# A Hymba-style decoder layer on one Trainium2 core: value stores and bias repeats on another queue, squares and reloads at other places

## The chip, the cores and the metric

The kernel is one program on one core of a Trainium2 chip. A core has a matrix engine (TensorE, PE in the profile), a vector engine (VectorE, DVE), a scalar engine (ScalarE, ACT), GpSimd (POOL) and SyncE (SP). Each of them runs its own list of instructions in order and waits on semaphores for the others. Transfers between the chip's memory (HBM) and on-chip memory are issued from an engine's list too: here from SP's and from ACT's ("SPq" and "ACTq" in the profile). The transfers themselves run beside the engines.

The metric is the device time of one execution in microseconds (us). The kernel before has a median of 2388.04 us over 3 runs (2383.22 to 2388.99).

## What is computed

One layer of a decoder over 2048 tokens of width 1024, in float32: a root-mean-square norm, one joint projection, two kinds of heads side by side (gated linear attention, and dilated windowed attention with a relative position bias), an output projection, and a feed-forward with squared ReLU.

```python
nx = rmsnorm(h, attn_norm_g)
gq, gk, gv, gr, glow, dq, dk, dv = split(nx @ w_in)          # widths 256,256,512,512,16,512,512,512
o_a = gla_mixer(gq, gk, gv, log_sigmoid(glow @ gla_gate_w2 + b) / 16)   # 4 heads
o_a = rmsnorm_per_head(o_a) * gla_norm_g * silu(gr)
o_b = dilated_mixer(dq, dk, dv, rel_bias)                    # 8 heads, (128,1) (512,4) (2048,16)
h = h + concat([o_a, o_b]) @ w_out
a = square(relu(rmsnorm(h, mlp_norm_g) @ w_ff1))             # 1024 -> 4096
h = h + a @ w_ff2                                            # 4096 -> 1024
y = rmsnorm(h, final_norm_g)
```

## The kernel before

**How a large product is made.** Every float32 operand is split into a high part of reduced precision (`hi`, written by ACT) and the rest (`lo`, by DVE), and a product is three matmuls (`mm3`, lines 66 to 69: high × high, low × high, high × low). On top of that, each large matrix product is cut 2 × 2 and made by Strassen's scheme in Winograd's form: seven products of sums of quarters in place of eight, taken in the order 1, 2, 5, 6, 3, 4, 7. The sums of the tokens' quarters are made once and kept on chip as `TF[j]` (j is the number of the product), a high and a low tile of 128 × 2048 each; those of the weights are made just before use. In the projections every product is left in one of four PSUM banks taken in rotation, and ACT, DVE and POOL carry it into accumulators (`acc` tiles; `CX`, `c11`, `c12`, `c21`, `c22` are their halves).

**Projections (lines 149 to 521, about the first 580 us).** A job is a pair (g, j): 18 groups of seven jobs, 126 jobs. The nine column groups are, in order, `dv`, `gr`, `dq`, `dk`, `dq`, `dk`, `gq`, `gk`, `gv`; groups 0 to 8 are for the first 1024 tokens, 9 to 17 for the second. Groups `dv`, `gr` and `gv` have 256 or 264 columns in each half, and a job is four products (i = 0 to 3, one for each 128 tokens) of 12 matmuls; the others have 128 columns, and a job is one product of 12 matmuls of 512 columns.

- `load_w` (185) asks on SP for a quarter of the next group's weights (tiles `wraw`) as soon as POOL has finished with the old one; `prep` (202 to 214) makes the high and low part (`wcomb`) two jobs ahead of the product, and POOL the sums.
- `product` (275) issues the matmuls; its `rest` evicts (lines 302 to 319); `finish` (235) post-processes a finished quarter and stores it. q and k of the windows go to `qD` and `kD` from ACT (250), q and k of the linear attention from ACT (243), the gates on SP. The values of the windows go to `vD` and, in another arrangement, to `vN`, those of the linear attention to `gvD` (268 to 271): one store for each 128 tokens and column half, on SP for group 0 and on ACT for all others.
- The first 1024 tokens are normalised, transposed and summed at the start. The second 1024 are made ready in the course of groups 1 to 7 by the generator `second_half` (410 to 435), one step each time the job loop meets a number of the list `OTHER` (36). It has four rounds (two blocks of 128 tokens each), and a round has five steps: two loads of x (tile `xp`); two squares on ACT (420), the inverse root and the scaling on DVE (422); the transposes on PE and their evictions by ACT (378, 426) of the first block, and of the second; the sums on DVE and seven stores to `nTD` on SP (429 to 434). `OTHER` puts these steps at jobs 7, 9, 10, 11, 12 in the first round and in the others at jobs 0, 4, 7, 8, 9 counted from the first job of groups 2, 4 and 6 (jobs 14, 28 and 42). All rounds share the tiles `xp` and `bp`.
- In group 8 `reload` (437) brings each of the seven sums back from `nTD` into `xp` or `bp` in turn, and one split (345 on ACT, 346 on DVE; 128 × 2048) rewrites `TF[j]` after its last use by the first half's tokens. Then `bias_rows` (325) makes the relative bias of each distance as one row per head and dilation in `rowD`, in the same tiles.
- `spread_bias` (338) repeats such a row 128 times from `rowD` to `rbD`, two heads at a time: twelve transfers of 384 KB, issued on ACT, at every third job from 72 to 105. The attention reads `rbD` (line 565).

**What sets the order.** The job loop stands under `manual_schedule` for PE, DVE, ACT and POOL. The builder still moves single instructions ahead of work that was written before them; `tc.keep_in_program_order` forbids that for one instruction: it stays behind whatever was written before it on its engine. SP's list and everything outside the block (attention, feed-forward) are ordered by the framework's scheduler. Each transfer signals one of eight completion semaphores in turn, whichever engine issues it, and its issue waits for the transfer before it on the same semaphore.

**Feed-forward.** After the attention (to about 1040 us) and the output projection, whose last row tiles already feed the next norm (`norm_to_T`, which stores the seven sums of transposed rows to `hTD`), the first feed-forward runs (1160 to 1760 us): 32 groups of seven jobs (`jobs1`), 16 groups of columns for the first half of the tokens and 16 for the second, each job 12 matmuls of 512 columns. `reload` (1018) brings a sum from `hTD` into a ring `rb` of tiles and returns a function that splits it into `TF[j]`. The first three (`RELOAD`) are asked for among the output projection's row tiles, the fourth just before the job loop, the next ones each when the one before has been split. The ring has one tile, and a second from the third job on. At the turn to the second half (group 15, jobs 105 to 111) each job is followed by one whole split of its j, and by the request for the load two places on. All large tiles come from one ring of 25 slots (`slot`).

Of the kernel before, what the change touches and what calls it, by code (L numbers as in the profile page):

```python
# [13 lines left out]
AF = mybir.ActivationFunctionType  # L14
# [4 lines left out]
D = 1024  # L19
# [13 lines left out]
XG = (6, 7)  # L33
XSC = {0: (3,), 1: (4,), 2: (5,), 3: (), 4: (6,)}
TOP = (5,)
OTHER = [7, 9, 10, 11, 12] + [14 * k + n for k in (1, 2, 3) for n in (0, 4, 7, 8, 9)]
G0, GE = 8, 56
RELOAD = (10, 11, 12)
BANKS = {"a": 2, "c": 3, "d": 2, "o": 1}
# [2 lines left out]
def emit(tc, a, stop=99):  # L42
    nc = tc.nc
    V, A, G, T, SP = nc.vector, nc.scalar, nc.gpsimd, nc.tensor, nc.sync
# [9 lines left out]
    def slot(name, dt=F32, n=SLOT):  # L54

        return up.tile([128, SLOT], dt, name=name, tag="u", bufs=25)[:, :n]
# [14 lines left out]
    def token_rows(ap, c, row, width=D):  # L71

        return bass.AP(tensor=ap.tensor, offset=ap.offset + c * 128 * row,
                       ap=[[row, 16], [16 * row, 8], [1, width]])

    A.preload_act_table_set("natural_log_exp_and_others")
    ident = const.tile([128, 128], F32, name="ident")
# [54 lines left out]
    gvD = dram.tile([S, 512], F32, name="gvD")  # L132
# [4 lines left out]
    vD = dram.tile([S, 512], F32, name="vD")  # L137
    vN = dram.tile([S, 512], F32, name="vN")
# [3 lines left out]
    hTD = dram.tile([2, 7, 128, 4, 512], F32, name="hTD")  # L142
# [3 lines left out]
    rbD = [dram.tile([8, 128, 384], F32, name=f"rbD{d}") for d in range(3)]  # L146
# [10 lines left out]
    xp, bp, acc = slot("xp"), slot("bp"), [slot("acc") for _ in range(3)]  # L157
# [14 lines left out]
    order = (1, 2, 5, 6, 3, 4, 7)  # L172
# [62 lines left out]
    def finish(g, n, k, i):  # L235

        kind, c0, w = groups[g % NG]
        tb = 2 * (g // NG) + k
        c = C[n][k]
        if w == 128:  # L240
            tk = slice(512 * tb, 512 * tb + 512)
            if kind in ("gq", "gk"):
                A.dma_start((gqD if kind == "gq" else gkD)[n, :, tk], c[:, :512])
                return
            pr = (c0 - (DQ if kind == "dq" else DK)) // 128 + n
            hi = c[:, 512:1024].bitcast(FR)
            A.activation(hi, c[:, :512], AF.Copy)
            V.tensor_tensor(c[:, :512], c[:, :512], hi.bitcast(F32), op=OP.subtract)
            for part in range(2):
                A.dma_start((qD if kind == "dq" else kD)[pr][:, part, tk], c[:, 512 - 512 * part:1024 - 512 * part])  # L250
            return
        t = 4 * tb + i
        tk = slice(t * 128, t * 128 + 128)
        s = c[:, i * w:i * w + w]
        if kind == "gr":
            j = n * w
            m = min(w, 512 - j)
            sg = stage()[:, :m]
            log_sigmoid(sg, s[:, :m])
            A.activation(sg, sg, AF.Exp)  # L260
            V.tensor_tensor(s[:, :m], sg, s[:, :m], op=OP.mult)
            G.tensor_tensor(s[:, :m], s[:, :m], gnB[:, j:j + m], op=OP.mult)
            SP.dma_start(srD[tk, j:j + m], s[:, :m])
            if m < w:
                gate(s[:, m:w], t)
            return
        j = n * w
        q = SP if g == 0 else A
        q.dma_start((vD if kind == "dv" else gvD)[tk, j:j + w], s)
        if kind == "dv":  # L270
            q.dma_start(token_rows(vN[:, j:], t, 512, w), s)

    banks = [0]

# [63 lines left out]
    def spread_bias(d, h):  # L338

        row = rowD[h:, d]  # L340
        A.dma_start(rbD[d][h:h + 2].rearrange("h p n -> p h n"),
                    bass.AP(tensor=row.tensor, offset=row.offset, ap=[[0, 128], [3 * 384, 2], [1, 384]]))

    def split(hi, lo, src):
        A.activation(hi, src, AF.Copy)  # L345
        V.tensor_tensor(lo, src, hi.bitcast(F32), op=OP.subtract)  # L346
# [22 lines left out]
        for cs in (slice(0, 512), slice(512, D)) if t == 0 else (slice(0, D),):  # L369
            V.scalar_tensor_tensor(xs[t][:, cs], x_src(t)[:, cs], X[t], gB[:, cs], op0=OP.mult, op1=OP.mult)  # L370

    def transposed(xt, last=None):
        out = []
        for q in range(2):
            pv = view(ps("cd"[q]), (4, 128))
            for k in range(4):
                of = xt[:, (4 * q + k) * 128:(4 * q + k + 1) * 128]
                T.transpose(pv[:, k, :], last if last is not None and 4 * q + k == 7 else of, ident)
            out.append(pv)
        return out  # L380

# [28 lines left out]
    def second_half():  # L410

        b = [view(bp[:, 512 * q:], (4, 128)) for q in range(4)]
        for i in range(4):
            for k in range(2):
                x_load(8 + 4 * k + i, xp[:, D * k:D * k + D])
            yield
            for k in range(2):
                xt = xp[:, D * k:D * k + D]
                ss = stat()
                A.activation(bp[:, :D], xt, AF.Square, accum_out=ss)  # L420
                r = rstd_of(ss, D)
                V.scalar_tensor_tensor(xt, xt, r, gB, op0=OP.mult, op1=OP.mult)
            yield
            for k in range(2):
                for q, pv in enumerate(transposed(xp[:, D * k:])):
                    A.activation(b[2 * k + q], pv, AF.Copy)
                yield
            (b11, b21, b12, b22), (t2, t4, t3) = b, [view(xp[:, 512 * q:], (4, 128)) for q in range(3)]
            V.tensor_tensor(b12, b12, b11, op=OP.subtract)
            V.tensor_tensor(t2, b22, b12, op=OP.subtract)  # L430
            V.tensor_tensor(t4, b21, t2, op=OP.subtract)
            V.tensor_tensor(t3, t2, b11, op=OP.subtract)
            for j, v in ((1, b11), (2, b21), (5, b12), (6, t2), (3, b22), (4, t4), (7, t3)):
                SP.dma_start(nTD[j - 1][:, :, i * 128:i * 128 + 128], v)
            yield

    def reload(j):
        t = (xp, bp)[order.index(j) % 2][:, :2048]
        SP.dma_start(t, nTD[j - 1].rearrange("p c s -> p (c s)"))
        return lambda: split(*[v[:, :2048] for v in TF[j]], t)  # L440
# [574 lines left out]

    turns = [0]

    def reload(j, half):

        t = rb[turns[0] % len(rb)][:, :2048]  # L1020
        turns[0] += 1
        SP.dma_start(t, hTD[half, j - 1].rearrange("p c s -> p (c s)"))

        def rest():
            if j not in TF:
                TF[j] = [slot(f"hb{j}", FR) for _ in range(2)]
                TB[j] = [view(v, (4, 512)) for v in TF[j]]
            split(*[v[:, :2048] for v in TF[j]], t)

        return rest  # L1030

    def mix_T(t):
        u = view(slot("mx"), (2, D))
# [100 lines left out]
    for at, t in enumerate(tiles):  # L1134
        u, m = nxt
        if at + 1 < NT:
            nxt = mix_T(tiles[at + 1])
        h = u[:, 1]
        p = [ps("a"), ps("a")]
        parts_ = 2 if at < 2 else 1  # L1140
        for q in range(parts_):
            for n in range(2):
                cs = slice(n * 512, n * 512 + 512)
                for c in range(q * CH // parts_, (q + 1) * CH // parts_):
                    mm3(p[n], m[:, 0, c], m[:, 1, c], WO[c][:, 0, cs], WO[c][:, 1, cs], c == 0, c == CH - 1)
                if q == parts_ - 1:
                    V.tensor_tensor(h[:, cs], p[n], u[:, 1, cs], op=OP.add)
        SP.dma_start(hD[t * 128:t * 128 + 128], h)
        if late is not None:
            norm_to_T(*late)  # L1150
        if back:
            back.pop()()
        if at in RELOAD:
            back.append(reload(order[at - RELOAD[0]], 0))
        if at == W1AT:
            load_w1(0)
        if at == W1AT + 1:
            prep1(0)
            prep1(1)
        late = (h, u[:, 0], t)  # L1160
# [123 lines left out]
        tk = slice(i * 128, i * 128 + 128)  # L1284
        mm3(p, l[:, 0, c, tk], l[:, 1, c, tk], r[:, 0, c], r[:, 1, c], n % 8 == 0 and c == 0, n % 8 == 7 and c == 1)

    back = [*back, reload(order[len(RELOAD)], 0)]
    load_w1(1)
    for at in range(7):
        if at == 2:  # L1290
            norm_to_T(*late)
            rb.append(slot("rb"))
        if back:
            back.pop(0)()
        if len(TF) < 7 and not back:
            back.append(reload(order[len(TF)], 0))
        prep1(at + 2)
        product1(at)
    for at in range(7, len(jobs1)):
        if at in (7 * NP - 9, 7 * NP - 8):  # L1300
            back.append(reload(order[at - 7 * NP + 9], 1))
        prep1(at + 2)
        product1(at)
        if jobs1[at][0] == NP - 1:
            back.pop(0)()
            if at + 2 < 7 * NP:
                back.append(reload(order[at + 2 - 7 * NP + 7], 1))
        if at == len(jobs1) - 6:
            for n in range(2):
                load_b(n)  # L1310
                load_a(n)
        if at in (len(jobs1) - 4, len(jobs1) - 2):
            n = (at + 4 - len(jobs1)) // 2
            prep_b(n)
            prep_a(n)
# [81 lines left out]
```

## Time and profile before

| quantity | value |
| --- | --- |
| median of 3 runs | 2388.04 us (2383.22 to 2388.99) |
| the profiled execution's own time | 2389.83 us |
| its span, first to last instruction | 2388.0 us |
| mean granted clock of TensorE | 0.989 |
| DMA | 458.13 MB, mean 192 GB/s |
| PE busy in the projections, 0 to 580 | 528.2 us |
| PE busy in 1500 to 1750 (feed-forward, second half) | 250.00 us of 250 |

The profile is one execution on the chip. A row of waits reads "engine line waited for: us in total, times, longest"; a row of the timeline has the start, the duration, the engine (SPq and ACTq are issues of transfers), the line and the operation "out<-in", and in brackets the idle time before it and what ended it. A row for a line or a tile gives durations in ns (min/median/max), the first and the last start, and the forms; "DMA to landing" is the time from the issue of a transfer to its end. In the rows of windows stand the stretch, its length, PE's busy time with the number of its instructions, the granted clock (1.00 is full), the mean busy share of the 16 DMA engines, and what they moved.

### The profile page before, as it was taken

How to read it: one execution, taken by the hardware profiler on the slowest of the kernel's cores; microseconds unless marked ns; L12 is line 12 of the kernel's file. 1: busy time of each engine (PE TensorE's matmuls, PEld its weight loads, DVE VectorE, ACT ScalarE, POOL GpSimd, SP SyncE). 2: the span in 40 equal slices, each digit the busy share in tenths (PEclk: the TensorE clock that was granted, in tenths of full speed). 3: DMA queues.
4: the chain of work that ended last, by engine and by line, in shares of the span. 5: the costliest groups of instructions: out<-in, count | busy, mean ns of one | idle time of the engine just before them, and what ended most of it. 6: DMA issues, size and time to landing. Idle time of an engine off the chain costs nothing.

```text
span 2388.0 us, 35096 instructions
## 1 busy us (share of the span) xinstructions
PE 2306.9 (97%) x12648; PEld 1988.7 (83%) x12648; DVE 1563.7 (65%) x2879; ACT 1147.0 (48%) x2181; POOL 582.9 (24%) x551
## 2 busy tenths in 40 slices
PE   6999998999999999999999999999999999999998
PEld 5877898779999988888788887888888888888887
DVE  6887675765677778445777778777773455456555
ACT  5565434633766766223555556555553333224323
POOL 5555434546584675100000000000000100001002
PEclk9999999999999999999999999999999999999999
DMA  6457664556667657568654447544467496547653
GB/s 159 122 161 235 202 195 139 194 168 206 207 202 252 208 161 245 172 206 273 202 191 146 154 159 246 178 158 150 146 221 272 150 308 211 175 163 247 218 167 106
DMA packets 342156, 458.13 MB, mean 192 GB/s; under 512 B 19236, under 2 KB 215349, under 8 KB 335710
## 3 DMA queue, kind: packets, MB, share of 16 engines
q1 hardware_dynamic: 313230, 413.15, 53.8%
q10 hardware_dynamic: 28752, 42.74, 5.2%
q8 instruction: 99, 1.62, 0.3%
q14 instruction: 75, 0.61, 0.1%
HBM read 293.51 MB, written 167.02 MB: 193 GB/s over the span
## 4 chain that ended last, share of the span: by engine, by line
PE 73%; DVE 8%; DMA 7%; issue 5%; POOL 3%; ACT 3%; ACTq 0%; SPq 0%; POOLq 0%; DVEq 0%
PE ps_a L67 8%; PE ps_a L68 8%; PE ps_a L69 8%; PE ps_c L67 7%; PE ps_c L69 7%; PE ps_c L68 7%; PE ps_d L67 4%; PE ps_d L68 4%; PE ps_d L69 4%; PE ps_o L67 3%; PE ps_o L68 3%; PE ps_o L69 3%; PE ps_a L674 3%; PE ps_d L655 2%; PE ps_c L633 1%
## 5 line engine op out<-in xcount | busy, mean ns | idle before, releaser
L1231 POOL TENSOR_TENSOR suma<-suma,gs 128x512 f32<-128x512 f32 x16 | 23.3, 1473 | 1149.4 <-ACT scr L1229 1149.3
L346 DVE TENSOR_TENSOR ca<-ra,ca 128x1024 fp32r<-128x1024 f32 x112 | 137.7, 1231 | 157.5 <-ACT ca L345 157.5
L345 ACT ACTIVATE ca<-ra 128x1024 fp32r<-128x1024 f32 x112 | 117.7, 1052 | 216.8 <-PE ps_c L69 167.3
L345 ACT ACTIVATE w1comb<-w1raw 128x512 fp32r<-128x512 f32 x224 | 139.5, 626 | 159.3 <-PE ps_c L69 57.8
L646 ACT ACTIVATE pe<-pe,O 128x256 f32<-128x256 f32 (+1 forms) x384 | 155.8, 454 | 73.7 <-DVE O L645 60.5
L674 PE MATMUL ps_a<-v,pt 128*128 128x65 f32 x1200 | 183.1, 255 | 7.7 <-DVE pt L664 6.6
L674 PEld LDWEIGHTS ps_a<-v,pt 128*128 128x128 f32 x1200 | 178.8, 198 | 11.4 <-DVE pt L664 8.3
L346 DVE TENSOR_TENSOR w1comb<-w1raw,w1comb 128x512 fp32r<-128x512 f32 x224 | 153.9, 690 | 51.3 <-ACT w1comb L345 51.0
L655 PE MATMUL ps_d<-ident,pe 128*128 128x128 f32 x600 | 161.5, 283 | 0.5 <-ACT pe L646 0.5
L645 DVE CUSTOM_DVE_ANT_0 pe<-ps_c,nb 128x256 f32<-128x256 f32 (+1 forms) x384 | 126.1, 361 | 39.5 <-PE ps_d L655 17.9
L202 ACT ACTIVATE wcomb<-wraw 128x512 fp32r<-128x512 f32 (+2 forms) x126 | 96.3, 773 | 110.0 <-PE ps_a L69 21.9
L204 DVE TENSOR_TENSOR wcomb<-wraw,wcomb 128x512 fp32r<-128x512 f32 (+2 forms) x84 | 99.9, 1194 | 71.6 <-ACT wcomb L202 71.4
L345 ACT ACTIVATE cb<-rb 128x1024 fp32r<-128x1024 f32 x56 | 59.4, 1061 | 168.7 <-PE ps_o L68 99.2
L67 PE MATMUL ps_c<-hb,w1comb 128*128 128x512 f32 x336 | 131.7, 392 | 2.4 <-ACT hb L345 2.4
L68 PE MATMUL ps_c<-hb,w1comb 128*128 128x512 f32 x336 | 131.6, 392 | 1.0 <-DVE w1comb L346 1.0
L69 PE MATMUL ps_c<-hb,w1comb 128*128 128x512 f32 x336 | 131.1, 390 | 0.0
L67 PE MATMUL ps_c<-cb,ca 128*128 128x512 f32 x336 | 130.8, 389 | 0.0
L68 PE MATMUL ps_c<-cb,ca 128*128 128x512 f32 x336 | 130.8, 389 | 0.0
L69 PE MATMUL ps_c<-cb,ca 128*128 128x512 f32 x336 | 130.8, 389 | 0.0
L655 PEld LDWEIGHTS ps_d<-ident,pe 128*128 128x128 f32 x600 | 112.0, 191 | 1.0 <-ACT pe L646 0.7
L94 POOL TENSOR_TENSOR stats<-stats,mhalf 128x1 f32<-128x1 f32 (+1 forms) x64 | 47.2, 743 | 254.1 <-DVE stats L93 208.9
L346 DVE TENSOR_TENSOR cb<-rb,cb 128x1024 fp32r<-128x1024 f32 x56 | 68.2, 1223 | 61.0 <-ACT cb L345 60.9
(351 smaller groups left out, 7342.4 us busy)
## 6 DMA issues: line engine op xcount, KB each, us to landing
ra<-actD SPq DMA_DIRECT2D x56, 1024.0 KB, 6.8
actD<-acc SPq DMA_DIRECT2D x192, 256.0 KB, 2.3
rb<-w_ff SPq DMA_DIRECT2D x72, 512.0 KB, 4.8
w1raw<-w_ff SPq DMA_DIRECT2D x32, 1024.0 KB, 7.6
k<-kD SPq DMA_DIRECT2D x16, 1024.0 KB, 8.9
rb<-hTD SPq DMA_DIRECT2D x14, 1024.0 KB, 5.7
wraw<-w_in SPq DMA_DIRECT2D x48, 256.0 KB, 3.3
boD<-O SPq DMA_DIRECT2D x8, 1056.0 KB, 4.5
```

Source lines behind the costliest of these rows:

```text
L67: T.matmul(out, sh, mh, start=first, stop=False)
L68: T.matmul(out, sl, mh, start=False, stop=False)
L69: T.matmul(out, sh, ml, start=False, stop=last)
L94: G.tensor_tensor(r2, r, mhalf[:, :n], op=OP.pow)
L202: A.activation(hi, src, AF.Copy, scale=sc)
L204: V.tensor_tensor(lo, src, hi.bitcast(F32), op=OP.subtract)
L345: A.activation(hi, src, AF.Copy)
L346: V.tensor_tensor(lo, src, hi.bitcast(F32), op=OP.subtract)
L645: V.tensor_tensor_reduce(p, s, bias, scale=1.0, scalar=BIG, op0=OP.add, op1=OP.min, accum_out=nm)
L646: A.activation(p, p, AF.Exp, bias=nm, scale=-1.0)
L655: T.transpose(pb[:, i * 128:i * 128 + 128], src, ident)
L674: T.matmul(self.b.opsum[:, n % 4], self.pt[:, i * 128:i * 128 + 128], self.b.v[:, blk, cols], start=first, stop=last)
```

## The change

In the projections:

- The squares, and the first transpose of each block in `second_half`, are kept in program order. `OTHER` puts the steps of rounds 2 to 4 at jobs 0, 6, 9, 10, 11 in place of 0, 4, 7, 8, 9.
- The values' second arrangement `vN` is still stored per 128 tokens, now always on SP. `vD` and `gvD` are stored once for four blocks (512 tokens, 512 KB), after the fourth, on SP.
- The twelve repeats of the biases are issued on SP and kept in program order there.

In the first feed-forward:

- The second tile of the ring and a further tile (`rt`) exist before the job loop; the fourth, fifth and sixth reload are asked for before it, the seventh after the second job's split.
- A split is two halves of 1024 columns. At the turn the fourteen halves are spread over jobs 106 to 116, the n-th at job 106 + 4n/5; the first two loads are asked for at job 103, and that of place k + 2 after the second half of place k.

```diff
-OTHER = [7, 9, 10, 11, 12] + [14 * k + n for k in (1, 2, 3) for n in (0, 4, 7, 8, 9)]
+OTHER = [7, 9, 10, 11, 12] + [14 * k + n for k in (1, 2, 3) for n in (0, 6, 9, 10, 11)]
...
-        q = SP if g == 0 else A
-        q.dma_start((vD if kind == "dv" else gvD)[tk, j:j + w], s)
         if kind == "dv":
-            q.dma_start(token_rows(vN[:, j:], t, 512, w), s)
+            SP.dma_start(token_rows(vN[:, j:], t, 512, w), s)
+        if i == 3:
+            SP.dma_start((vD if kind == "dv" else gvD)[512 * tb:512 * tb + 512, j:j + w].rearrange("(i p) n -> p i n", i=4),
+                         c[:, :4 * w].rearrange("p (i n) -> p i n", i=4))
...
-        A.dma_start(rbD[d][h:h + 2].rearrange("h p n -> p h n"),
-                    bass.AP(tensor=row.tensor, offset=row.offset, ap=[[0, 128], [3 * 384, 2], [1, 384]]))
+        tc.keep_in_program_order(
+            SP.dma_start(rbD[d][h:h + 2].rearrange("h p n -> p h n"),
+                         bass.AP(tensor=row.tensor, offset=row.offset, ap=[[0, 128], [3 * 384, 2], [1, 384]])))
...
-    def transposed(xt, last=None):
+    def transposed(xt, last=None, pin=False):
...
-                T.transpose(pv[:, k, :], last if last is not None and 4 * q + k == 7 else of, ident)
+                ins = T.transpose(pv[:, k, :], last if last is not None and 4 * q + k == 7 else of, ident)
+                if pin and q + k == 0:
+                    tc.keep_in_program_order(ins)
...
-                A.activation(bp[:, :D], xt, AF.Square, accum_out=ss)
+                tc.keep_in_program_order(A.activation(bp[:, :D], xt, AF.Square, accum_out=ss))
...
-                for q, pv in enumerate(transposed(xp[:, D * k:])):
+                for q, pv in enumerate(transposed(xp[:, D * k:], pin=True)):
...
-    def reload(j, half):
+    def reload(j, half, t=None):
-
-        t = rb[turns[0] % len(rb)][:, :2048]
-        turns[0] += 1
-        SP.dma_start(t, hTD[half, j - 1].rearrange("p c s -> p (c s)"))
+        if t is None:
+            t = rb[turns[0] % len(rb)]
+            turns[0] += 1
+        SP.dma_start(t[:, :2048], hTD[half, j - 1].rearrange("p c s -> p (c s)"))
...
-            split(*[v[:, :2048] for v in TF[j]], t)
-
-        return rest
+            for cs in (slice(0, 1024), slice(1024, 2048)):
+                split(*[v[:, cs] for v in TF[j]], t[:, cs])
+                yield
+
+        return rest()
...
-    back = [*back, reload(order[len(RELOAD)], 0)]
+    rb.append(slot("rb"))
+    back = [*back, reload(order[3], 0), reload(order[4], 0), reload(order[5], 0, slot("rt"))]
...
-            rb.append(slot("rb"))
         if back:
-            back.pop(0)()
-        if len(TF) < 7 and not back:
-            back.append(reload(order[len(TF)], 0))
+            list(back.pop(0))
+        if at == 1:
+            back.append(reload(order[6], 0))
...
+    first, parts_at = 7 * (NP - 1), {}
+    for n in range(14):
+        parts_at.setdefault(first + 1 + n * 4 // 5, []).append(n // 2)
+    halves, begun = {}, set()
     for at in range(7, len(jobs1)):
-        if at in (7 * NP - 9, 7 * NP - 8):
-            back.append(reload(order[at - 7 * NP + 9], 1))
+        if at == first - 2:
+            halves.update({n: reload(order[n], 1) for n in range(2)})
...
-        if jobs1[at][0] == NP - 1:
-            back.pop(0)()
-            if at + 2 < 7 * NP:
-                back.append(reload(order[at + 2 - 7 * NP + 7], 1))
+        for n in parts_at.get(at, ()):
+            next(halves[n])
+            if n in begun and n + 2 < 7:
+                halves[n + 2] = reload(order[n + 2], 1)
+            begun.add(n)
```

More of the change, by code (lines that the diff above doesn't have):

```diff
@@ L1151, in emit @@
         if back:
-            back.pop()()
+            list(back.pop())
         if at in RELOAD:
```

## The prediction

> **What bounds the kernel now.** I read the page first, then busy time by stage, then the losses in short windows, then what each late instruction waited for.
>
> ```profile
> span 2388.0 us, 35096 instructions
> PE 2306.9 (97%) x12648; PEld 1988.7 (83%) x12648; DVE 1563.7 (65%) x2879; ACT 1147.0 (48%) x2181; POOL 582.9 (24%) x551
> 60.00:580.00 520.00, 489.64 (x2948) 0.98 0.59 177
> 580.00:1160.00 580.00, 564.66 (x4137) 0.99 0.67 215
> 1160.00:1760.00 600.00, 595.11 (x2614) 1.00 0.51 171
> 1760.00:2388.00 628.00, 618.98 (x2729) 1.00 0.61 205
> ```
>
> In a window row stand the stretch, its length, PE's busy time with its instructions, the granted clock, the DMA share and GB/s. PE sets the time everywhere: 2306.9 of 2388.0 us. The change leaves its matmuls alone, so only PE's losses can move: idle time, and busy time at a lowered clock. The projections after their start (60 to 580) idle 30.4 us, the first feed-forward (1160 to 1760) 4.9. For a shorter window I count the loss as idle time plus busy time times (1 − clock).
>
> ```profile
> 130.00:150.00 20.00, 17.82 (x65) 0.83 0.39 100
> 210.00:215.00 5.00, 2.94 (x17) 1.00 0.75 262
> 235.00:245.00 10.00, 6.68 (x22) 0.66 0.59 194
> 280.00:290.00 10.00, 8.13 (x66) 1.00 0.47 139
> 320.00:335.00 15.00, 12.16 (x98) 1.00 0.42 125
> 360.00:385.00 25.00, 16.44 (x107) 0.80 0.77 227
> 385.00:390.00 5.00, 5.00 (x43) 1.00 0.29 74
> 445.00:460.00 15.00, 12.94 (x54) 1.00 0.64 199
> 1165.00:1180.00 15.00, 12.55 (x48) 0.89 0.66 206
> 1465.00:1480.00 15.00, 12.56 (x54) 1.00 0.68 253
> ```
>
> The losses are, in order: 2.18 + 17.82 × 0.17 = 5.2; 2.06; 3.32 + 6.68 × 0.34 = 5.6; 1.87; 2.84; 8.56 + 16.44 × 0.20 = 11.8; none at 385, which shows the full pace of 256-wide matmuls (43 in 5 us, 0.116 us each); 2.06; 2.45 + 12.55 × 0.11 = 3.8; 2.44 us. Their causes, by the views of waits:
>
> ```profile
> ACT bp L420 <- DMA xp<-x: 15.7, 6, 5.3
> PE ps_c L378 <- DVE xp L422: 2.1, 1, 2.1
> PE ps_d L378 <- DVE stats L93: 3.3, 1, 3.3
> 133.69 1.06 ACT L420 ACTIVATE bp<-xp 128x1024 f32<-128x1024 f32 x1 [3.34 <-DMA xp<-x]
> ```
>
> The first, second and third windows are one thing: ACT runs in order and stands at a square whose tokens are still landing (15.7 us in six waits); the evictions and weight preparations behind it are late, and so are the scaled rows that PE transposes.
>
> ```profile
> PE ps_c L67 <- ACT wcomb L202: 5.2, 1, 5.2
> PE ps_o L67 <- ACT acc L315: 3.3, 1, 3.3
> ACT wcomb L202 <- DMA vN<-acc: 11.9, 1, 11.9
> ACT acc L315 <- DMA vD<-acc: 9.1, 1, 9.1
> L341 ACTq DMA_DIRECT2D rbD<-rowD x12: 538/608/1131, 350.2 to 380.0; - x12
> DMA to landing us min/median/max: 4.6/7.9/13.6
> ```
>
> The waits of PE and ACT in 345 to 385 and the repeats' own view. The window at 360 is ACT's queue of transfers: all twelve bias repeats are issued between 350.2 and 380.0 us among the second token half's value stores, each takes 7.9 us (median) to land, and a value store that must wait for an earlier landing holds ACT for 9.1 and 11.9 us. PE then waits 5.2 and 3.3 us, and its clock falls.
>
> ```profile
> PE ps_c L67 <- ACT hb L345: 2.4, 1, 2.4
> PE ps_d L67 <- ACT hb L345: 1.3, 1, 1.3
> ACT hb L345 <- DMA rb<-hTD: 5.3, 3, 3.9
> ```
>
> At 1165 and 1465 PE waits for whole splits (ACT hb) of reloaded operands, some of whose loads had not landed.
>
> **The change, part by part.** It removes 48 transfers: 64 stores of attention and GLA values, 128 rows each, become 16 of 512 rows. In the built program ACT's transfers go from 189 to 113, SP's from 1013 to 1041; bytes and PE's instructions stay.
>
> 1. Squares. In the built order the squares of the second token group go from position 124 of ACT's list to 195, those of the fourth from 256 to 268 (about seven products, some 20 us), while their loads stay; those of the third keep their place, but its loads come about 6.7 us earlier, since the transposes ahead of them do. The waits were 3.34 and up to 5.3 us, well below both shifts, so the losses 5.2 + 2.1 + 5.6 = 12.9 us can go. The bound on the gain is 12.9. From the other side: the pinned transposes sit in PE's order, where nothing overtakes them, so a late row now stops PE itself; I keep half, 6, as the poor end. I take −11, near the full end, as 20 us stands against 5.3.
>
> 2. Value stores and repeats off ACT. The two ACT waits can't arise on ACT any more; bound 11.8. Before the wait DVE and ACT were already close behind PE, so I take −10.5; poor end −8.5, PE's two waits alone.
>
> 3. Where the repeats go. They now stand on SP at every third product, some 380 to 520 us, each beside weight loads and q and k stores.
>
> ```profile
> L565 SPq DMA_DIRECT2D nb<-rbD x24: 319/427/538, 549.2 to 593.8; - x24
> L250 ACTq DMA_DIRECT2D qD<-acc x16: 326/326/475, 428.3 to 492.7; - x16
>   ACT acc L307: 5.6, 2
> DMA to landing us min/median/max: 2.0/3.5/6.0
> SPq L185 <- POOL wraw L210: 30.8, 4, 14.1
> ```
>
> These are the first reads of the repeats, the views of tile qD from 400 to 580 (who waited for it, its landings), and SP's waits from 200 to 300. ACT L307 overwrites a tile that a q store is reading; it waited 5.6 us in two cases, and the 445 window lost 2.06. With repeats in the same stretch these landings lengthen. Of twelve repeats perhaps four meet a q or k pair at up to 2.06 us each: 0 to +8. I take +3, three at half of that. SP itself stands up to 14.1 us before a weight load until POOL frees the raw tile, so a repeat or value store behind it waits too; nothing needs a repeat before its reads at 549 us. The tiles behind the joined value stores are written again two to three jobs later (a job of four 256-wide products is 48 matmuls of 0.116 us, 5.6 us), so they have 11 us; cover gone, ACT waits as above.
>
> The Trainium skill, "DMA: Bandwidth & Descriptors", section "Issuing engines are not separate DMA queues", says that transfers started by any of the engines share the same 16 DMA engines, and that spreading the issuing saves only the issue time. By that alone part 2 would gain nothing beyond ACT's issues; the waits for landing (9.1 and 11.9 us) speak against it here, since they block evictions, which on SP's queue they do not.
>
> 4. Later transposes. The fourth group's transposes come 42 matmuls later than before (0.225 us each at 512 columns, as in the row of 1500 below): 9.4 us for its seven stores and for the reloads of group 8 behind them.
>
> ```profile
> 270.05 0.34 SPq L439 DMA_DIRECT2D xp<-nTD  x1
> 282.31 1.94 ACT L345 ACTIVATE tb<-xp 128x2048 fp32r<-128x2048 f32 x1
> 279.63 1.06 ACT L202 ACTIVATE wcomb<-wraw 128x1024 fp32r<-128x1024 f32 x1 [7.51 <-POOL wraw L208]
> xp<-nTD SPq DMA_DIRECT2D x4, 1024.0 KB, 7.9
> ```
>
> The reload at 270.05 moves to about 279.5 (SP's queue adds some 2: 282), lands near 288, and its split stands in ACT's order right behind the evictions that ended at 282.3 less the wraw wait: up to 8.5 us of ACT held. PE rotates four banks, three products (12 × 0.116 us each) ahead of an eviction, 4.2 us; with the hold at 7, as the place on SP is known to some 2 us: +3. Ends 0 (the split slides without stopping PE) and +6 (half clock too).
>
> 5. Weight loads of group 8 now stand ahead of the fourth group's stores on SP; ACT's 7.51 us wait on the raw weights goes, with the 1.87 us window. −1.9, ends 0 and −1.9. The 320 window (DVE with splits) is untouched, and a later chain gives it less room; 0, in the range of part 4.
>
> 6. First feed-forward, start. Two more tiles hold reloads, three are requested before the first product instead of one after the other: the 3.8 us window goes but for the split's own time. −3, ends 0 and −3.8 (the extra tiles come out of the same ring of 25, and could delay the last row tile's load or the second weight tile).
>
> 7. Turn of the halves. Splits come as fourteen halves over eleven products instead of seven whole ones over seven.
>
> ```profile
> DMA to landing us min/median/max: 4.8/6.7/8.5
> 1500.00:1750.00 250.00, 250.00 (x1105) 1.00 0.46 156
> ```
>
> The landings are those of the reloads from 1440 to 1510. A product is 12 × 250/1105 = 2.71 us. ACT and DVE are freed between halves, but a load is asked for only two or three products (5.4 to 8.1 us) ahead of its first half, against landings of 4.8 to 8.5: an ACT wait of up to 3 us stays. −1.5, ends −2.4 and +1.
>
> Attention, the output projection and the second feed-forward keep their order: 0.
>
> Sum: −11 − 10.5 + 3 + 3 − 1.9 − 3 − 1.5 = −21.9. The profiled execution took 2389.83 us (span 2388.0), 1.8 above the runs' median of 2388.04: 2389.8 − 21.9 = 2367.9, and I say 2367.5. All good ends: −12.9 − 11.8 + 0 + 0 − 1.9 − 3.8 − 2.4 = −32.8, 2357. All poor ends: −6 − 8.5 + 8 + 6 + 0 + 0 + 1 = +0.5, 2390.
>
> **Rivals.**
>
> A. Everything gained, nothing new: −30 to −33, about 2358. For it: the repeats have some 30 us to spare, and the split could slide. Against: the later reload has a chain of its own (stores, load, split) that the rows show without slack. 15%.
>
> B. The squares' stall only moves to the reload: ACT held 8.5 us at 288, PE through its banks, then at half clock as in the 235 window (2.3 us): +8.5 + 2.3 = 11 instead of 3. −21.9 + 8 = −14, 2376. For it: reloads and splits are chained through two tiles. Against: PE's bank slack. 14%.
>
> C. The transfers decide, not the queue: repeats at 7.9 us hold back whatever they meet, so part 2 is given back as waits elsewhere. −21.9 + 10.5 = −11.4, 2378.5. Against it: in 360 to 385 the DMA share was 0.77, not full, and what waited there was ACT's order. 10%. The Trainium skill's rule on shared DMA engines (part 3) would have it come out this way.
>
> D. Slower: SP becomes the blocked queue. A transfer that must wait for an earlier one's landing held ACT; the same wait now holds SP, whose next entry is a weight load. Each repeat would cost one late load (the 280 window, 1.87) and one late q or k store (half of 2.06): 12 × 2.9 = 35 in place of part 3's 3: −21.9 + 32 = +10, 2400. It decides where SP's hold exceeds the lead of the weight loads, which are asked for most of a group ahead (seven products, 19 us at 128 columns); the longest landing of a repeat was 13.6 us, seen with eight in flight, so I doubt it. 7%.
>
> E. The edits don't take, and the scheduler's order swallows them. The built order shows them moved; only the feed-forward part could vanish. 2% for nothing.
>
> **Chances.** The forecast, −16 to −27, has 52%; A to E as above. This kernel's measurement tells about 0.3% (7 us) from no change. Faster by more than that: all of the forecast and A, most of B and C: 0.84. Within: the rest of B and C, and E: 0.08. Slower: D and mishaps of its kind: 0.08. The range leaves out D and A's edge: 2356 to 2385; the likeliest one's own is 2362 to 2374.
>
> **What would show it.** Right: in 130 to 245 no wait of ACT for xp<-x above 1 us and PE busy in the 5 us windows there; between 350 and 385 no ACT wait on a value store's landing; PE at clock 1.00 near 370; PE full at 1165 to 1180. Part 4: ACT waiting for xp<-nTD near 288. Part 3: ACT L307 waiting for q or k stores at 400 to 520, more than 5.6 us in all. D: POOL waiting for wraw loads there, and SP's queue held at repeats. It would be wrong if 60 to 580 idles as much as before at other places, or if a stage that I set to 0 (attention) moves.

## The result and the profile after

The changed kernel takes 2374.87 us (median of 4 runs, 2372.88 to 2376.36), the kernel before 2388.51 us in the runs beside it. The ratio is 0.9944 with a 95% interval of 0.9923 to 0.9965: about 13.6 us faster, where 20.5 were forecast. The profiled execution has a span of 2374.6 us, 13.4 below that of before. The measured time lies in the range of 2356 to 2385, but just beyond the 2362 to 2374 that were called likeliest.

PE's list holds 9168 matmuls of lines 67 to 69 in every kernel here. The builder lets some of them change places, but over a few products only: in the projections each window below holds the same matmuls, by line and bank, in every kernel (but for four at job 70 in e1). At the limits in the feed-forward up to 11 are exchanged for others of the same shape. So windows can be cut at the i-th matmul, which is the same amount of work in each trace. The first fence has such windows of the kernel before, the second those of the changed kernel. Row by row they are the jobs from 14 to 21, 21 to 27, 27 to 35, 35 to 42, 42 to 49, 49 to 70, 70 to 77, 77 to 90, 90 to 98, 98 to 105, then the first 14 jobs of the first feed-forward and its jobs 103 to 120. The length is what matters here.

```profile
130.37:158.71 28.34, 25.92 (x101) 0.88 0.46 132
158.71:178.90 20.19, 19.80 (x86) 1.00 0.63 202
178.90:203.45 24.55, 24.55 (x110) 1.00 0.70 216
203.45:226.80 23.35, 21.30 (x102) 1.00 0.82 243
226.80:253.06 26.26, 22.94 (x94) 0.87 0.66 189
253.06:362.64 109.58, 104.86 (x771) 1.00 0.67 208
362.64:416.08 53.44, 44.88 (x340) 0.90 0.47 136
416.08:459.82 43.74, 41.68 (x177) 1.00 0.55 171
459.82:483.53 23.71, 23.71 (x101) 1.00 0.71 239
483.53:505.02 21.49, 19.59 (x85) 1.00 0.54 171
1150.87:1194.43 43.56, 41.11 (x179) 0.96 0.64 205
...
1436.51:1486.07 49.56, 47.12 (x205) 1.00 0.67 232
```

```profile
130.75:154.65 23.90, 22.35 (x95) 1.00 0.59 165
154.65:175.30 20.65, 20.03 (x86) 1.00 0.56 178
175.30:209.02 33.72, 27.67 (x117) 0.95 0.68 191
209.02:231.61 22.59, 21.11 (x101) 1.00 0.71 216
231.61:250.75 19.14, 19.14 (x86) 1.00 0.76 227
250.75:362.45 111.70, 107.05 (x780) 0.98 0.62 195
362.45:404.28 41.83, 41.38 (x340) 1.00 0.41 117
404.28:446.33 42.05, 41.43 (x176) 1.00 0.66 202
446.33:476.56 30.23, 26.41 (x103) 0.94 0.76 236
476.56:499.20 22.64, 20.27 (x85) 1.00 0.66 200
1145.05:1184.19 39.14, 39.14 (x179) 1.00 0.87 279
...
1426.27:1473.65 47.38, 46.57 (x205) 1.00 0.66 233
```

Read the lengths against each other. At the stalls that the change aimed at, time was gained: 4.4 us at jobs 14 to 21, 0.8 at 35 to 42 and 7.1 at 42 to 49 (squares), 11.6 at 70 to 77 (ACT's queue), 4.4 and 2.2 in the feed-forward. ACT has no wait for x left between 60 and 300 us. But two stretches that were at full pace have become slow: jobs 27 to 35 take 9.2 us more, jobs 90 to 98 take 6.5 more.

The first of the two, by PE's waits from 182 to 202 us and the timeline of DVE (start, duration, line), first in the changed kernel, then two rows of the one before:

```profile
PE ps_o L67 <- DVE acc L305: 3.7, 1, 3.7
```

```profile
188.90 1.78 DVE L320 TENSOR_TENSOR acc<-acc 128x512 f32<-128x512 f32 x1
190.60 1.78 DVE L434 TENSOR_TENSOR xp<-bp 128x512 f32<-128x512 f32 x1
192.42 1.65 DVE L435 TENSOR_TENSOR xp<-bp,xp 128x512 f32<-128x512 f32 x1
193.99 0.68 DVE L436 TENSOR_TENSOR xp<-xp,bp 128x512 f32<-128x512 f32 x1
194.59 1.28 DVE L248 TENSOR_TENSOR acc<-acc 128x512 f32<-128x512 f32 x2
195.79 1.00 DVE L305 TENSOR_TENSOR acc<-ps_o,acc 128x512 f32<-128x512 f32 x1
```

```profile
188.83 1.02 DVE L304 TENSOR_TENSOR acc<-ps_o,acc 128x512 f32<-128x512 f32 x1
...
197.29 1.79 DVE L430 TENSOR_TENSOR xp<-bp 128x512 f32<-128x512 f32 x1
```

Line 305 is the eviction (304 before) of the bank that PE needs. In DVE's list it now stands behind the last three sums of the second token group (434 to 436, places 210 to 212, the eviction at 215). Before, it stood ahead of them (place 210, the sums, then lines 430 to 432, at 219 to 221). The group's squares start some ten products later than they did (at 170.80 us, 133.69 before) and the first of its four sums about five; these three come about two products earlier. PE stands 3.7 us and then runs at a lowered clock (0.95 over the window). The same holds in every kernel here: the seven with the sums ahead of this eviction take 32.8 to 35.1 us for jobs 27 to 35, the seven with the sums behind it 24.6 to 25.5.

The second, by the waits of ACT and PE of the changed kernel from 455 to 495 us, and then the landings of k's transfers (tile kD) from 400 to 580, first in the changed kernel, then in the one before:

```profile
ACT acc L308 <- DMA kD<-acc: 5.6, 1, 5.6
...
ACT acc L308 <- DMA qD<-acc: 2.2, 1, 2.2
```

```profile
PE ps_o L67 <- ACT wcomb L202: 1.7, 1, 1.7
```

```profile
DMA to landing us min/median/max: 2.1/5.2/10.1
```

```profile
DMA to landing us min/median/max: 2.0/2.7/4.2
```

These transfers land in 5.2 us (median) in place of 2.7. One of those counted is a load of k; the stores alone, 11 and 10 of 16 with a landing on record, took 5.0 and 2.7. ACT, which overwrites the tile, stands 5.6 us for one of them, and PE waits for weights (wcomb) that ACT makes in the same order. The waits don't price each link of this chain; that the repeats set it off is shown by e1.

### The profile page after: what moved, and what is told of

Read it like the earlier page. It is cut to its first block, busy times and chain, and to the rows that moved or that the text cites. A ratio compares the mean times of both kernels' runs of the same rounds, so it can differ in the third digit from the quotient of the medians.

```text
span 2374.6 us, 35066 instructions
## 1 busy us (share of the span) xinstructions
PE 2303.8 (97%) x12648; PEld 1985.9 (84%) x12648; DVE 1563.5 (66%) x2893; ACT 1148.6 (48%) x2195; POOL 577.9 (24%) x551
## 4 chain that ended last, share of the span: by engine, by line
PE 80%; DVE 8%; DMA 4%; issue 4%; ACT 2%; POOL 2%; SPq 0%; ACTq 0%; POOLq 0%; DVEq 0%
PE ps_a L67 8%; PE ps_a L69 8%; PE ps_a L68 8%; PE ps_c L68 7%; PE ps_c L69 7%; PE ps_c L67 7%; PE ps_d L67 4%; PE ps_d L69 4%; PE ps_d L68 4%; PE ps_a L678 3%; PE ps_o L67 3%; PE ps_o L68 3%; PE ps_o L69 3%; PE ps_d L659 2%; PE ps_c L637 2%
## 5 line engine op out<-in xcount | busy, mean ns | idle before, releaser
L1238 POOL TENSOR_TENSOR suma<-suma,gs 128x512 f32<-128x512 f32 x16 | 23.3, 1472 | 1142.8 <-ACT scr L1236 1142.8
L67 PE MATMUL ps_a<-wcomb,tb 128*128 128x256 f32 (+1 forms) x336 | 99.1, 295 | 10.5 <-DVE acc L305 5.5
```

The costliest lines, as they stand in the source:

```text
L67: T.matmul(out, sh, mh, start=first, stop=False)
```

## The experiments

Times are medians; the kernel before ran beside each of them. The table has the length of each stretch of PE's list in the profiled execution, by jobs, in us; FF is the first 14 jobs of the first feed-forward, turn its jobs 103 to 120.

| kernel | median | 14-27 | 27-35 | 35-49 | 14-49 | 49-70 | 70-77 | 77-90 | 90-105 | FF | turn |
| --- | --- | --- | --- | --- | --- | --- | --- | --- | --- | --- | --- |
| before | 2388.5 | 48.5 | 24.6 | 49.6 | 122.7 | 109.6 | 53.4 | 43.7 | 45.2 | 43.6 | 49.6 |
| changed | 2374.9 | 44.6 | 33.7 | 41.7 | 120.0 | 111.7 | 41.8 | 42.1 | 52.9 | 39.1 | 47.4 |
| e1 | 2380.2 | 46.6 | 32.8 | 41.8 | 121.1 | 119.0 | 42.9 | 43.3 | 46.8 | 39.1 | 47.0 |
| e2 | 2379.0 | 44.5 | 34.8 | 41.7 | 121.0 | 110.5 | 43.4 | 42.1 | 53.5 | 39.9 | 47.1 |
| e3 | 2376.6 | 48.4 | 24.6 | 48.3 | 121.3 | 108.4 | 41.8 | 42.1 | 52.1 | 39.2 | 47.0 |
| e4 | 2374.7 | 47.4 | 25.5 | 44.7 | 117.5 | 112.1 | 41.8 | 42.1 | 51.3 | 39.3 | 47.0 |
| e5 | 2378.4 | 45.0 | 33.7 | 41.8 | 120.4 | 112.3 | 41.8 | 44.7 | 50.4 | 39.4 | 47.0 |
| e6 | 2372.6 | 48.8 | 25.5 | 43.3 | 117.6 | 111.7 | 41.7 | 42.0 | 52.0 | 39.5 | 47.0 |
| e7 | 2377.9 | 44.9 | 35.1 | 41.8 | 121.7 | 110.0 | 41.8 | 42.0 | 52.5 | 39.1 | 47.7 |
| e8 | 2384.0 | 45.0 | 33.6 | 44.7 | 123.2 | 109.2 | 41.8 | 42.1 | 51.7 | 45.2 | 49.1 |
| e9 | 2376.5 | 44.9 | 34.9 | 41.8 | 121.6 | 111.5 | 46.2 | 45.3 | 45.3 | 39.2 | 47.0 |
| e10 | 2375.5 | 45.8 | 25.4 | 47.6 | 118.8 | 111.6 | 45.2 | 45.1 | 46.7 | 39.1 | 47.0 |
| e11 | 2369.9 | 47.4 | 25.5 | 44.8 | 117.6 | 112.3 | 41.8 | 44.5 | 45.5 | 39.1 | 47.0 |
| e12 | 2371.0 | 49.0 | 25.4 | 44.4 | 118.8 | 111.9 | 41.7 | 43.2 | 45.3 | 39.1 | 47.0 |

### Repeats back on ACT (e1)

```diff
-        tc.keep_in_program_order(
-            SP.dma_start(rbD[d][h:h + 2].rearrange("h p n -> p h n"),
-                         bass.AP(tensor=row.tensor, offset=row.offset, ap=[[0, 128], [3 * 384, 2], [1, 384]])))
+        A.dma_start(rbD[d][h:h + 2].rearrange("h p n -> p h n"),
+                    bass.AP(tensor=row.tensor, offset=row.offset, ap=[[0, 128], [3 * 384, 2], [1, 384]]))
```

> The changed kernel (2374.9 us) with the twelve bias repeats back on ACT, not pinned; value stores stay joined on SP. Theory: the repeats are what held ACT at jobs 70 to 72 (their landings, 7.9 us median, against 2 for a value store), so most of the 12.3 us gained there is lost again (+8 to +12), while the 6 us lost at jobs 90 to 101, where q and k stores wait, come back: 2377 to 2381. Rival: the many value stores held ACT; then jobs 70 to 72 stay good and the 6 us come back: about 2369.

It took 2380.2 us. ACT's and PE's waits of this kernel from 320 to 400 us:

```profile
ACT acc L316 <- DMA rbD<-rowD: 11.8, 2, 9.7
```

```profile
PE ps_o L67 <- ACT acc L316: 6.7, 1, 6.7
```

With no value store on ACT's queue the repeats hold ACT by themselves, now a little earlier (jobs 49 to 70 lose 7.3 us, 70 to 77 lose 1.1). So 8.4 of the 11.6 us are lost again. Jobs 90 to 105 are back to 46.8. So the repeats are the cause of most of the old stall and, on SP, of the new one at jobs 90 to 105.

### Value stores back on ACT (e2)

```diff
+        q = SP if g == 0 else A
+        q.dma_start((vD if kind == "dv" else gvD)[tk, j:j + w], s)
         if kind == "dv":
-            SP.dma_start(token_rows(vN[:, j:], t, 512, w), s)
-        if i == 3:
-            SP.dma_start((vD if kind == "dv" else gvD)[512 * tb:512 * tb + 512, j:j + w].rearrange("(i p) n -> p i n", i=4),
-                         c[:, :4 * w].rearrange("p (i n) -> p i n", i=4))
+            q.dma_start(token_rows(vN[:, j:], t, 512, w), s)
```

> The changed kernel with the value stores as before (one for each 128 tokens, on ACT but for group 0), the repeats on SP. Theory: without repeats among them they land in about 2 us and hold ACT for little, also with 48 more transfers: 2374 to 2378, no ACT wait above 3 us between 345 and 385. Rival: the value stores themselves are the stall, which returns: 2384 to 2387.

2379.0 us. The stall does not return: jobs 70 to 77 take 43.4, 1.6 more, and ACT waits for no landing between 320 and 400. Its profiled execution, the longest of its five, is 6.8 us longer than the changed kernel's, and 5.3 of that lie in the attention (364.6 us against 359.3). That is above the scatter of this stage (last section), but the engines' lists in it are not quite those of the other kernels; what made it longer is not shown. Joining these stores is worth 1 to 2 us where they are made, which single profiles hardly tell from scatter.

### Squares undone (e3)

```diff
-OTHER = [7, 9, 10, 11, 12] + [14 * k + n for k in (1, 2, 3) for n in (0, 6, 9, 10, 11)]
+OTHER = [7, 9, 10, 11, 12] + [14 * k + n for k in (1, 2, 3) for n in (0, 4, 7, 8, 9)]
-                tc.keep_in_program_order(A.activation(bp[:, :D], xt, AF.Square, accum_out=ss))
+                A.activation(bp[:, :D], xt, AF.Square, accum_out=ss)
-                for q, pv in enumerate(transposed(xp[:, D * k:], pin=True)):
+                for q, pv in enumerate(transposed(xp[:, D * k:])):
```

> The changed kernel with the squares' and transposes' pins and the offsets as before. Theory from the two traces, job by job: part 1 gained 4.4 + 1.5 + 6.6 at jobs 15 to 20, 37 to 39 and 44 to 46, and lost 10.1 at jobs 27 to 32, so undoing it costs about 2 to 3 us: 2377, with PE full from 180 to 200 and the three old stalls back. Rival: the loss at jobs 27 to 32 comes from something else (the value stores on SP), and undoing costs the 11 us of the prediction: 2386.

2376.6 us, as the theory had it. Jobs 27 to 35 fall to 24.6, and the old stalls return. Jobs 14 to 49 differ by 1.3 us in all, not by 11, and that is within the scatter: the kernels that share the changed kernel's steps there (changed, e1, e2, e5, e8, e9) took 120.0 to 123.2.

### Pins with the old offsets (e4), and only round 2 at them (e6)

```diff
-OTHER = [7, 9, 10, 11, 12] + [14 * k + n for k in (1, 2, 3) for n in (0, 6, 9, 10, 11)]
+OTHER = [7, 9, 10, 11, 12] + [14 * k + n for k in (1, 2, 3) for n in (0, 4, 7, 8, 9)]
...
+OTHER = [7, 9, 10, 11, 12, 14, 18, 21, 22, 23] + [14 * k + n for k in (2, 3) for n in (0, 6, 9, 10, 11)]
```

> The changed kernel with the pins but the offsets 0, 4, 7, 8, 9. Theory: the pins alone end the waits for x (a load of about 7 us against four jobs, 10.9 us), and the loss at jobs 27 to 32 is round 2's four sums on DVE standing ahead of an eviction at the start of group 4; two jobs earlier they don't meet it: -5 to -10, 2365 to 2370. Rival: the pinned transposes themselves stop PE wherever they stand, and the time stays within 3 us of 2375; a second rival, that six products are needed because x lands late: ACT waits for xp<-x above 1 us and 2378 or more.

> The changed kernel, pins kept, with only the second round at the old offsets 0, 4, 7, 8, 9 (rounds 3 and 4 at 0, 6, 9, 10, 11). Theory: the stall at jobs 27 to 35 (9 us) belongs to round 2's sums on DVE two jobs later, the new stall at jobs 35 to 42 of the run with all offsets old (2.9 us) to round 3's squares two jobs earlier; so here 27 to 35 in 25.5 us, 35 to 42 in 22.6 us, 21 to 27 in 23.4: 5 to 6 us below the changed kernel in the profile, 2369. Rival: round 3's place depends on round 2's, and 35 to 42 loses 3 us all the same: 2372.

e4 took 2374.7 us by the median (2369.6 to 2380.6), no better than the changed kernel, though its profiled execution was 6.8 shorter. In its profile the stall at jobs 27 to 35 goes as the theory says (25.5), and ACT waits for x 2.6 us in two cases, 1.6 the longest (the fence below), against 15.7 us in six before: the second rival's wait is there, but small, and its time is not reached. But new losses come before and behind. PE's waits of e4 from 155 to 235 us:

```profile
PE ps_a L67 <- ACT wcomb L202: 3.1, 2, 2.8
PE ps_c L380 <- DVE xp L426: 3.0, 2, 2.8
```

ACT's waits of e4 from 60 to 300 us:

```profile
ACT bp L424 <- DMA xp<-x: 2.6, 2, 1.6
```

The pinned transposes now come before DVE has scaled their rows. e6 (2372.6 us) shows the same at round 2: 8 us gained at jobs 27 to 35, 4.2 lost at 14 to 27, 1.6 at 35 to 49. Jobs 35 to 42, where the theory had 22.6 us, took 23.3. Of five arrangements of these steps (changed, e3, e4, e6, e10) none takes jobs 14 to 49 below 117.5 us, 2.5 less than the changed kernel.

### Squares pinned alone (e7)

```diff
-                for q, pv in enumerate(transposed(xp[:, D * k:], pin=True)):
+                for q, pv in enumerate(transposed(xp[:, D * k:])):
```

> The changed kernel with the squares pinned but not the transposes. Theory: the waits for x stay gone (jobs 14 to 21 in 23.9 us, 42 to 49 in 19.1), and the scheduler spreads the transposes again, so the stall at jobs 27 to 35 shrinks by 3 us or more: 2366 to 2372. Rival: the DVE work of the later squares alone makes the stall, and 27 to 35 stays at 33 us: 2374 to 2376.

The rival holds: 35.1 us at jobs 27 to 35, with the same wait of 3.7 us for DVE's line 305, and 2377.9 us. The pinned transposes are not what stops PE there. What is left are the moved steps of round 2, as e6 shows, which put the three sums ahead of the eviction.

### Feed-forward as before (e8)

The functions and loops of the first feed-forward are those of the kernel before.

> The changed kernel with the first feed-forward's reloads as before. Theory: its start loses 4.4 us and its turn 2.2 us, nothing else moves: 2381 to 2382 by the median, 6.6 more in the profile. Rival: the gain at the start came from the earlier stages (the last row tiles), and only the turn's 2.2 us come back: 2377.

2384.0 us. The start loses 6.0, the turn 1.7, nothing else in the feed-forward moves: more than the 6.6 that the two traces showed, from the same places. Jobs 35 to 49 take 3.0 us more than in the changed kernel, with the same steps there: so much can a stretch differ from profile to profile.

### Repeats in the gate group, two a job (e5) and three a job (e9)

```diff
-        if 7 * NG + 8 <= at < 7 * NG + 44 and at % 3 == 0:
-            spread_bias(2 - (at - 7 * NG - 8) // 12, (at - 7 * NG - 8) // 3 % 4 * 2)
+        if 7 * NG + 8 <= at < 7 * NG + 14:                    # e9: < 7 * NG + 12, three in place of two
+            for n in (2 * (at - 7 * NG - 8), 2 * (at - 7 * NG - 8) + 1):
+                spread_bias(2 - n // 4, n % 4 * 2)
```

> The changed kernel with the twelve repeats, still on SP and pinned, two at each of jobs 71 to 76 (the gate group, which stores no q or k) in place of every third job from 72 to 105. Theory: the 6 to 7 us lost at jobs 90 to 101 come from repeats among q and k stores, so they go here (jobs 90 to 98 in 23.7 us, not 30.2), and the gate group, where the DMA share was 0.39, takes the repeats for less than 2 us: 2367 to 2370. Rival: it is the bytes and the queue wherever they stand (4.7 MB in 35 us): jobs 70 to 77 lose 5 us or more, by late weights behind the repeats on SP: 2373 or more.

> The changed kernel with three repeats at each of jobs 71 to 74, so that in the built list of SP all twelve stand ahead of the weight loads of the next groups (in the run with two a job the last two stood 25 entries later and were issued at 466 us). Theory: with no repeat left at 460 to 480, where 2 MB of k for the attention are already being loaded, jobs 90 to 105 take 45.5 us or less (52.9 in the changed kernel, 50.4 with two a job) and jobs 70 to 90 gain or lose under 2: 2368 to 2371. Rival: the k loads alone saturate the transfers there, or the gate group pays: within 2 us of 2375.

In e5 (2378.4 us) jobs 90 to 98 are at 23.7 us, as expected, and 70 to 77 pay nothing. But 77 to 90 and 98 to 105 give back 6.7. The last two repeats stand 30 places further down in SP's list (issued at 466.5 and 467.2 us) and fall among the attention's first loads of k (2 MB). The transfers issued in 460 to 485 (KB each, median us to landing), and POOL's waits of e5 from 455 to 495:

```profile
k<-kD SPq DMA_DIRECT2D x1, 1024.0 KB, 8.8
wraw<-w_in SPq DMA_DIRECT2D x3, 256.0 KB, 10.0
rbD<-rowD SPq DMA_DIRECT2D x2, 384.0 KB, 9.3
```

```profile
POOL wraw L208 <- DMA wraw<-w_in: 9.9, 1, 9.9
```

A weight load lands in 10.0 us here (median of three); over the projections of before it was 3.3. In e9 (2376.5 us) no repeat is left there, and jobs 90 to 105 take 45.3, as the theory had it; but the rival is right too, for the gate group pays 4.4 us and the next jobs 3.3. POOL's and PE's waits of e9 from 355 to 440:

```profile
POOL wraw L208 <- DMA wraw<-w_in: 20.6, 3, 14.7
```

```profile
PE ps_d L227 <- POOL acc L319: 3.8, 1, 3.8
```

Nine of the repeats (3456 KB) are issued within 10.5 us, from 381.0 us on. POOL then stands 14.7 us for a weight load, and a sum that the gates need is behind it in POOL's list.

### Three a job and another round 2 (e10)

```diff
+OTHER = [7, 9, 10, 11, 12, 14, 18, 22, 23, 24] + [14 * k + n for k in (2, 3) for n in (0, 6, 9, 10, 11)]
```

> As the run with three repeats a job, and round 2 at jobs 14, 18, 22, 23, 24: squares two products earlier, transposes and sums one earlier than in the changed kernel. In the built lists round 2's four evictions and last three sums then stand nearly where the kernel before had them (177 and 208 to 211 on DVE, in place of 192 and 198 to 200). Theory: jobs 27 to 35 take 25 us as before, without the old wait for x (14 to 21 in 24), and the transposes don't wait as at offset 7: 9 us or more off jobs 14 to 56, 2358 to 2363. Rival: stall for stall again, jobs 21 to 27 lose 4 and 35 to 42 lose 2: 2366 or more.

2375.5 us: the rival. Jobs 27 to 35 take 25.4 as expected, with less lost at 14 to 27 (45.8) than in e4 and e6, but 35 to 49 lose 5.9, and the three-a-job repeats cost about what they cost in e9.

### Repeats where nobody waits (e11, e12)

```diff
+        if 7 * NG + 8 <= at < 7 * NG + 12 or at in (106, 108, 110, 112):     # e11: 8 + 4; offsets of e4
+            m = at - 7 * NG - 8
+            for n in (2 * m, 2 * m + 1) if m < 4 else ((at - 106) // 2 + 8,):
+                spread_bias(2 - n // 4, n % 4 * 2)
...
+        if 104 <= at < 116:                                                  # e12: offsets of e4
+            n = at - 104
+            spread_bias(2 - n // 4, n % 4 * 2)
```

> Pins with all offsets 0, 4, 7, 8, 9; eight repeats, two at each of jobs 71 to 74, the last four at jobs 106, 108, 110, 112, beyond the q and k stores and the first k loads of the attention. Theory: repeats cost only where they meet other transfers that somebody waits for: two a job in the gate group cost nothing at jobs 70 to 77 (41.8 us), jobs 90 to 105 take 45.4, and 105 on stays at 78.8; with the offsets' 2 to 3 us in all 8 to 10 us off the changed kernel, 2365 to 2367. Rival: the eight still make a late weight load (jobs 77 to 90 in 44.7, as with twelve), leaving 5 to 7: 2368 to 2370.

> The same offsets, all twelve repeats one at each of jobs 104 to 115. Theory: in the changed kernel PE is full from 500 to 540 us at a DMA share of 0.5, no q or k store is left there, and the first read of a repeat comes at about 540; so jobs 70 to 90 as in the changed kernel (83.9 us), 90 to 105 in 45.4, 105 on at 79: 10 us off, 2364 to 2366. Rival: 384 KB in every 2.7 us (141 GB/s) beside 155 make the weights of groups 15 and 16 late, or the attention's first reads: 3 us or more lost after job 105, 2368 or more.

e11 took 2369.9 us (2367.3 to 2374.7; ratio to the kernel before 0.9931, 0.9918 to 0.9945), e12 2371.0 us (0.9933, 0.9921 to 0.9945). Both lie below the changed kernel's median by 4 to 5 us, but their intervals overlap its own (0.9923 to 0.9965), so the medians alone don't show that they are faster. In both, jobs 90 to 105 take 45.4 us, 7.5 less than in the changed kernel. e11 pays 2.4 at jobs 77 to 90, as its rival said; e12 pays 1.1 there and 1.5 behind job 105. So most of what the repeats cost was their place.

## Why the forecast was right, and where it was not

The direction, the places and most of the mechanisms were right: the profile of before told which stalls would go, and they went or shrank. The sum was 8 us too large. One of the prediction's own signs of being wrong came close: PE idles 27.0 us in 60 to 580, against 30.4 before, much of it at other places.

- **Part 1, the squares (−11), was mis-sized, and this is the step that failed.** The waits for x are gone, but jobs 14 to 49 gained 122.7 − 120.0 = 2.7 us, less than the poor end of 6, and undoing the edit (e3) costs 1.3, no more than the scatter of that stretch. The step set 20 us of delay against a wait of 5.3 and asked only whether the load would be there. It named what is late next only as "a late row now stops PE itself"; what came was another order of work, three sums ahead of an eviction on DVE (e7 shows that it was not the pinned transposes). DVE is busy for 106 of 141 us there (119 to 260), and every arrangement tried moved most of the stall elsewhere (e4, e6, e10). Nor was the delay the same for both: the second group's squares came 37 us later, those of the fourth 22.
- **Part 2, off ACT (−10.5), was right:** −11.6 at jobs 70 to 77. e1 and e2 tell its two halves apart: the repeats alone bring 8.4 back, the values 1.6.
- **Part 3, the repeats' new place (+3, up to +8), had the right mechanism and too small a size:** jobs 90 to 105 lost 7.7 and 77 to 90 gained 1.7. Between 400 and 580 us ACT's waits for q and k stores grew from 7.0 us (line 307) to 14.9 (line 308). The step didn't count the 2 MB of k that the attention loads in the same stretch, also before; no run takes these loads away, so their share is not shown.
- **Parts 4 and 5 (+3 and −1.9)** together were +2.1 (jobs 49 to 70, 109.6 to 111.7), within the scatter: the four kernels with the changed kernel's steps there (changed, e5, e8, e9) took 109.2 to 112.3. ACT did wait for the reloads, 12.5 us in six waits, and its wait of 7.5 us for raw weights fell to 2.4. e3, which takes the later transposes back, has 108.4, as part 4 would have it; the two are not shown apart more closely.
- **Parts 6 and 7 (−3 and −1.5)** came out at −4.4 and −2.2 in the profiles; e8 gave 6.0 and 1.7 back.

Part 1 missed by 8.3 us, part 3 by 3; parts 2, 6 and 7 were better by 3.2. Of the rivals, A (everything gained) fell with the two new stalls. B had the form of what happened, a stall moved rather than removed, but at jobs 27 to 35 and on DVE, not at the reload. C, the traffic decides, is half true: at ACT's queue it was false, since the queue's order was the harm; at jobs 90 to 105 it is what happened, as moving the repeats showed. There the rule of the Trainium skill, "DMA: Bandwidth & Descriptors", section "Issuing engines are not separate DMA queues", agrees with the trace: k stores issued on ACT landed in 5.0 us (median) rather than 2.7 while repeats went out on SP. D's chain, a repeat, a late weight load, PE, exists (e5, e9), but only with the repeats packed; spread out, it did not decide.

## What to carry to other kernels

An instruction that waits in order does harm by what stands behind it. Taking a wait away by moving work is therefore priced twice: by the wait that goes, and by what the moved work, and all that the builder moves with it, then stands ahead of in a busy list. Transfers that nobody waits for should be put where no other transfer is waited for; which queue issues them matters less, once the queue is not the one that evicts. A trace cut at equal places of the busiest engine's list shows where each edit gave and took, where medians of five runs scatter by several microseconds; but one trace is one execution, and here a stretch with the same steps differed by about 3 us (jobs 14 to 49, 49 to 70).

## What the runs showed of the hardware that was not expected

The attention stage, from the last projection matmul to the first of the output projection, took from 357.1 to 361.9 us in twelve profiled kernels in which PE, DVE and POOL ran the same lists in the same order (the changed kernel and all experiments but e2). Most of that appears in steps of about 1 to 5 us, at a few places of the stage. It limits what a median of a few runs can tell of the other stages, and no run here shows its cause.

A 512-wide addition on DVE took 0.68 us alone and up to 1.78 us at 189 to 192 us (lines 320 and 434 in the timeline above). POOL was adding during these (1.72 us from 188.41, 1.74 from 190.09, 1.60 from 191.91). Over the first 580 us of this trace, all 22 such additions between on-chip tiles with no POOL instruction beside them took 0.67 to 0.69 us, and the 38 with one beside them 0.67 to 1.79. So the slow ones come only with POOL at work; that the two hold each other up was not tested by a run of its own.
